# A hybrid attention block with a 2x2-block feed-forward: fewer block units, one adding transfer for each, and elementwise work moved from GpSimd to VectorE

## The chip, the core and the metric

The kernel runs on one core of a Trainium2 chip. It is one launch; its time is the device time of that core in microseconds (us). In the profile, PE is TensorE, DVE is VectorE, ACT is ScalarE, POOL is GpSimd and SP is the queue that issues most transfers. Each engine works through its own list of instructions; what stands behind a waiting one in that list is late with it.

## What is computed

One layer of a hybrid block on 512 tokens with 1024 channels, in fp32. Four mixers read the normed input, their outputs are gated and merged, and a gated feed-forward with 2816 hidden columns follows:

```
h = rms_norm(x, attn_norm);  proj = h @ w_in          # split into q, k, v, gates of four mixers
y_fox   = fox_attention(norm(fq), norm(fk), fv, ff)   # 4 heads, decayed causal softmax
y_conv  = cb * conv1d(cc * cu)                        # width 3, per channel
y_mlstm = sigmoid(mo) * norm(mlstm(mq, mk, mv, ...))  # 4 heads, chunks of 64
y_swa   = swa_attention(norm(sq), norm(sk), sv)       # 8 heads, window 128
merged  = sum over the four of sigmoid(gate_i) * (y_i @ w_i_out)
x = x + merged @ w_merge_out
h = rms_norm(x, ffn_norm)
x = x + (silu(h @ w_gate) * (h @ w_up)) @ w_down
```

## The kernel before

All tokens stand in the free dimension: a tile is 128 channels by 512 tokens. Every fp32 operand is split into a high part `hi` and a remainder `lo` (`split`: ACT copies `hi`, DVE subtracts for `lo`), and each product is made of three matmuls (`mm3`): hi by hi, hi by lo, lo by hi. A projection (`proj`) of 128 output columns is 8 such triples, 24 matmuls of 512 columns.

The weights are one stream `w_str` of tiles of 128 x 1024 fp32 in the order of use. SP loads them into six buffers `wraw`; `w_split` splits each into `whi`/`wlo` (four buffers each, so two or three tiles ahead of their use).

The order of the program is: token projections `psn` on the raw input with the sums of squares `ssq`; `fk`, `fq` of the fox mixer (on `xg`, the input times the norm's gain, without the norm's factor); the conv mixer's `pcu`, `pcc`, `pcb` (on `xn`, the normed input, made by `normed_input`); the eight gate and output pairs of conv (`gconv`, `oconv`) with the fox attention mixed in; `sk`, `sq` of the window mixer, each normed per head (`head_normed`); `gfox`/`ofox` with the window attention mixed in; `pmv`, `pmk`, `pmq`, `pmo`; `gswa`; `gmlstm`; the merge `mg`; and the feed-forward. Attention runs as a background generator: `tick`, called once for each triple, advances it every `pace["period"]` triples. Projections and outputs share four PSUM buffers (`ps_mm`), taken in turn: `gconv` of the first output block takes the buffer that `pcb` of p = 0 held, and so waits until that has been read.

The feed-forward has 22 units of 128 hidden columns. A direct unit (`plain_unit`, the first three) is two projections, 48 matmuls of 512 columns. A block unit (the other 19) sees K (two halves), tokens (two halves) and gate/up as a 2x2 block product and makes it with 7 half products instead of 8: 7 x 4 x 3 = 84 matmuls of 256 columns (`product`). Its four weight sums t1 to t4 come from transfers that add as they write: `ff_load` adds into `ta` (t1 and t3), `ff_t2` copies t1 on ACT and adds a third tile into the copy, `ff_t4` copies t2 on ACT and adds a fourth. These adding transfers are issued from POOL (`accum_op`). After units 0 to 7, 8 to 14 and 15 to 21 follows the down product of that part (`dn`): eight output blocks, each a sum over the part's units, times `r2`, added to `x2`. The tile scheduler places the instructions of each engine; its order is what the compiled program has.

The head of the kernel's tuning that the change touches, and the product of a block unit:

```
PLAIN = 3
...
PARTS = ((0, 8), (8, 7), (15, 7))
...
def product(ps, w, a, start, stop):
    for k in range(4):
        wb = slice(k * P, (k + 1) * P)
        (wh, wl), (ah, al) = w, left[a][k]
        nc.tensor.matmul(ps, wh[:, wb], ah, ...)
        nc.tensor.matmul(ps, wh[:, wb], al, ...)
        nc.tensor.matmul(ps, wl[:, wb], ah, ...)
```

## Time and profile before

| | us |
|---|---|
| median of 3 runs | 864.37 (861.04 to 865.3) |
| the profiled execution's own time | 867.11 |
| its span, first to last instruction | 865.4 |
| PE busy / DVE busy / ACT busy / POOL busy | 835.9 / 593.1 / 429.0 / 225.9 |

The span is 1.7 us shorter than the execution's own time; the profiled execution is 2.7 us above the median. PE's busy time is not a measure of its pace: matmuls overlap, so a stretch is PE at its pace only if the starts of its matmuls stand as close as they can. The mean granted clock of TensorE was 0.99 of full speed.

### The profile page before, as it was taken

What the parts mean: (1) busy time and instruction counts of PE and PEld (TensorE: products, weight loads), DVE (VectorE), ACT (ScalarE), POOL (GpSimd) and SP (SyncE); (2) the same over time, 40 slices, a digit from 0 to 9 for tenths busy, and PEclk for the clock granted to TensorE, in tenths of its full rate; (3) what the DMA queues carried; (4) which work ended last, traced back from release to release, by engine and by line L of the source; (5) the groups of instructions that cost most, each with busy time, mean ns of one, the idle gap of its engine ahead of it and who ended that gap; (6) DMA issues with size and microseconds to landing.
All of it is one profiled execution on the core that took longest, in us unless ns stands there. A gap on an engine that the chain in (4) does not pass through costs nothing.

```text
span 865.4 us, 12163 instructions
## 1 busy us (share of the span) xinstructions
PE 835.9 (97%) x4563; PEld 722.0 (83%) x4563; DVE 593.1 (69%) x933; ACT 429.0 (50%) x704; POOL 225.9 (26%) x220
## 2 busy tenths in 40 slices
...
GB/s 317 175 123 112 84 74 74 98 127 43 84 88 86 147 85 51 96 87 167 184 119 173 123 75 119 199 182 181 131 147 183 204 212 109 158 191 159 86 56 86
DMA packets 47215, 112.36 MB, mean 130 GB/s; under 512 B 4991, under 2 KB 8616, under 8 KB 47156
## 3 DMA queue, kind: packets, MB, share of 16 engines
...
q14 instruction: 23, 0.19, 0.1%
...
## 4 chain that ended last, share of the span: by engine, by line
PE 77%; DVE 8%; ACT 4%; DMA 4%; issue 3%; POOL 3%; SPq 0%; ACTq 0%; DVEq 0%; POOLq 0%
PE dn L136 5%; PE dn L134 5%; PE dn L135 5%; DMA fta<-in_w_str_dram 3%; PE fa L922 2%; DVE fl L140 2%; PE fc L921 2%; PE fc L920 2%; PE fc L922 2%; PE fa L920 2%; PE gswa L134 2%; PE fa L921 2%; PE gswa L135 2%; PE gswa L136 2%; PE gmlstm L134 2%
## 5 line engine op out<-in xcount | busy, mean ns | idle before, releaser
L140 DVE TENSOR_TENSOR wl<-wr,wh 128x1024 fp32r<-128x1024 f32 x79 | 106.9, 1353 | 40.2 <-ACT wh L139 37.5
L139 ACT CAST wh<-wr 128x1024 fp32r<-128x1024 f32 x79 | 82.7, 1047 | 60.3 <-PE gconv L135 8.6
L135 PE MATMUL dn<-al,dh 128*128 128x512 f32 x176 | 68.4, 389 | 0.0
L136 PE MATMUL dn<-ah,dl 128*128 128x512 f32 x176 | 68.0, 390 | 0.0
L134 PE MATMUL dn<-ah,dh 128*128 128x512 f32 x176 | 67.2, 389 | 0.0
L139 ACT CAST dh<-dr 128x896 fp32r<-128x896 f32 (+1 forms) x24 | 23.1, 977 | 55.9 <-DMA dr<-in_w_str_dram 18.8
L140 DVE TENSOR_TENSOR fl<-fr,fh 128x1024 fp32r<-128x1024 f32 x19 | 39.4, 2072 | 9.5 <-ACT fh L139 9.5
L922 PE MATMUL fc<-lh,fl 128*128 128x256 f32 x152 | 43.4, 285 | 2.1 <-DVE fl L140 2.1
L1005 POOL TENSOR_TENSOR ut<-ut,gt 128x512 f32<-128x512 f32 x19 | 30.2, 1591 | 54.5 <-DVE ut L1003 45.6
L140 DVE TENSOR_TENSOR dl<-dr,dh 128x896 fp32r<-128x896 f32 (+1 forms) x24 | 35.6, 1488 | 12.9 <-ACT dh L139 12.9
L920 PE MATMUL fc<-lh,fh 128*128 128x256 f32 x152 | 43.3, 285 | 0.6 <-ACT fh L139 0.6
L921 PE MATMUL fc<-ll,fh 128*128 128x256 f32 x152 | 43.3, 285 | 0.0
L920 PE MATMUL fb<-lh,fh 128*128 128x256 f32 x152 | 43.2, 285 | 0.0
L921 PE MATMUL fb<-ll,fh 128*128 128x256 f32 x152 | 43.1, 284 | 0.0
L922 PE MATMUL fb<-lh,fl 128*128 128x256 f32 x152 | 43.0, 284 | 0.0
L1049 DVE TENSOR_TENSOR o<-dn,r 128x512 f32<-128x512 f32 (+1 forms) x25 | 16.3, 666 | 35.1 <-PE dn L136 35.1
L136 PEld LDWEIGHTS dn<-ah,dl 128*128 128x128 f32 x176 | 33.0, 188 | 7.3 <-DVE dl L140 0.5
L135 PEld LDWEIGHTS dn<-al,dh 128*128 128x128 f32 x176 | 33.1, 188 | 6.7
L134 PEld LDWEIGHTS dn<-ah,dh 128*128 128x128 f32 x176 | 33.1, 188 | 6.6
L139 ACT CAST fh<-fr 128x1024 fp32r<-128x1024 f32 x19 | 19.9, 1047 | 27.5 <-PE fc L921 23.9
L1051 POOL TENSOR_TENSOR x<-x,o 128x512 f32<-128x512 f32 x16 | 27.6, 1734 | 22.4 <-DVE o L1049 22.4
L819 POOL DMA_DIRECT2D fta<-in_w_str_dram x19 | 17.4, 939 | 61.4 <-DMA fta<-in_w_str_dram 36.7
...
## 6 DMA issues: line engine op xcount, KB each, us to landing
...
fr<-in_w_str_dram SPq DMA_DIRECT2D x19, 256.0 KB, 3.2
fr<-in_w_str_dram POOLq DMA_DIRECT2D x19, 256.0 KB, 5.4
ftb<-in_w_str_dram POOLq DMA_DIRECT2D x19, 256.0 KB, 5.6
...
```

The lines of the kernel that those rows point to most:

```text
L134: nc.tensor.matmul(out, a[0], b[0], start=start, stop=False)
L135: nc.tensor.matmul(out, a[0], b[1], start=False, stop=False)
L136: nc.tensor.matmul(out, a[1], b[0], start=False, stop=stop)
L139: nc.scalar.copy(hi, src)
L140: nc.vector.tensor_tensor(lo, src, hi.bitcast(F32), op=ALU.subtract)
L819: nc.gpsimd.dma_start(ta, src[1].rearrange("p (i c) -> p i c", i=2), accum_op=ALU.add)
L920: nc.tensor.matmul(ps, wh[:, wb], ah, start=start and k == 0, stop=False, skip_group_check=True)
L921: nc.tensor.matmul(ps, wh[:, wb], al, start=False, stop=False, skip_group_check=True)
L922: nc.tensor.matmul(ps, wl[:, wb], ah, start=False, stop=stop and k == 3, skip_group_check=True)
L1005: nc.gpsimd.tensor_tensor(ut, ut, gt, op=ALU.mult)
L1049: nc.vector.tensor_tensor(o[:, c:c + n], ps[:, c:c + n], r2[:, c:c + n], op=ALU.mult)
L1051: nc.gpsimd.tensor_tensor(x2[d], x2[d], o, op=ALU.add)
```

## The change

- Of the 22 feed-forward units 13 are block units (W) and 9 direct (P), in four parts `PPPWWP`, `WWPWWP`, `WWPWW`, `PWWPW`; the down product follows each part, so there are 32 down blocks instead of 24, each over 6 or 5 units.
- A block unit has one adding transfer (into `ta`). t2 and t4 are sums on DVE (`src_t2`, `src_t4`); the two ACT copies and two adding transfers go.
- All weights, those of block units and of the down product too, go through one list of jobs, loaded up to six buffers ahead and split by `w_split`.
- Elementwise work of POOL goes to DVE: the sums of squares, the products by the norm, the gated sums `acc`, `ut * gt`, `x2 + o`, and half of the sums of the left blocks. The copies for the second half of a key stack go the other way, from DVE to a transfer issued by POOL (`k_stack`).
- The conv projections read `xg` (the norm's factor is applied later, `r_sq` and `rb_`), so the normed input is first needed by `gconv`, and its making is spread over more steps. The high part of a squared head comes from a second ACT square.
- The fox attention starts after the conv projections, and goes on through the projections of the window mixer.

The diff, cut to what is spoken of:

```diff
-PLAIN = 3
+PARTS = ("PPPWWP", "WWPWWP", "WWPWW", "PWWPW")
...
+    def load_b2(f):
+        def go(raw):
+            src = w_str[FF0 + 2 * f:FF0 + 2 * f + 2]
+            ta[f] = big.tile([P, 2, NT], F32, tag="ysw", name=f"fta{f}", bufs=4)
+            nc.sync.dma_start(ta[f], src[:, :, 0:NT].rearrange("i p c -> p i c"))
+            nc.sync.dma_start(raw.rearrange("p (i c) -> p i c", i=2), src[:, :, NT:].rearrange("i p c -> p i c"))
+            nc.gpsimd.dma_start(ta[f], src[1].rearrange("p (i c) -> p i c", i=2), accum_op=ALU.add)
+        return go
+    def src_t2(f, i):
+        def go():
+            raw = stream["raw"][i + 1]
+            nc.vector.tensor_tensor(raw[:, NT:], ta[f][:, 0], stream["raw"][i][:, NT:], op=ALU.add)
+            return raw
+        return go
+    def src_t4(f, i):
+        def go():
+            t = wk(f"ftb{f}")
+            nc.vector.tensor_tensor(t, stream["raw"][i + 1][:, NT:], stream["raw"][i][:, 0:NT], op=ALU.add)
+            return t
+        return go
...
+    f = 0
+    for part in PARTS:
+        f0 = f
+        for kind in part:
+            if kind == "P":
+                add_whole(FF0 + 2 * f)
+                add_whole(FF0 + 2 * f + 1)
+            else:
+                i = len(loads)
+                loads += [load_b2(f), load_b11(f)]
+                jobs += [(i, src_t2(f, i), 2), (i, lambda f=f: ta[f].rearrange("p i c -> p (i c)"), 2),
+                         (i, src_raw(i), 2), (i, src_t4(f, i), 1)]
+            f += 1
+        for d in range(KO):
+            jobs.append((len(loads), src_raw(len(loads), (f - f0) * P), 0))
+            loads.append(load_cols((d * FB + f0) * P, (f - f0) * P))
...
-            nc.gpsimd.tensor_tensor(ssq, ssq, sq, op=ALU.add)
+            nc.vector.tensor_tensor(ssq, ssq, sq, op=ALU.add)
...
-        nc.gpsimd.tensor_tensor(t, t, rb_, op=ALU.mult)
+        nc.vector.scalar_tensor_tensor(
+            t, t, col[:, C_AN + ko:C_AN + ko + 1], rb_, op0=ALU.mult, op1=ALU.mult)
         h, l = s_tile(f"xnh{ko}", F32R), s_tile(f"xnl{ko}", F32R)
-        scaled_split(h, l, t, col[:, C_AN + ko:C_AN + ko + 1])
+        split(h, l, t)
         xn.append((h, l))
...
-            nc.vector.tensor_copy(a[oth], a.bitcast(F32)[own])
+            nc.gpsimd.dma_start(a[oth], a[own])
             nc.vector.tensor_tensor(b[own], src[own], a.bitcast(F32)[own], op=ALU.subtract)
-            nc.vector.tensor_copy(b[oth], b.bitcast(F32)[own])
+            nc.gpsimd.dma_start(b[oth], b[own])
...
-        nc.vector.tensor_copy(h, sq)
-        nc.gpsimd.tensor_tensor(l, sq, h.bitcast(F32), op=ALU.subtract)
+        if src is None:
+            nc.vector.tensor_copy(h, sq)
+        else:
+            nc.scalar.activation(h, src, AF.Square)
+        nc.vector.tensor_tensor(l, sq, h.bitcast(F32), op=ALU.subtract)
...
-        nc.gpsimd.tensor_tensor(qg, qg, sq, op=ALU.mult)
+        nc.vector.tensor_tensor(qg, qg, sq, op=ALU.mult)
...
-        ps = proj(f"pcu{p}")
+        ps = proj(f"pcu{p}", xg)
         u = wk(f"cu{p}")
-        nc.scalar.copy(u, ps)
-        ps = proj(f"pcc{p}")
+        nc.vector.tensor_tensor(u, ps, r_sq, op=ALU.mult)
+        ps = proj(f"pcc{p}", xg)
         z = wk(f"cz{p}")
         nc.vector.tensor_tensor(z, ps, u, op=ALU.mult)
-        if p == 0:
-            pace["period"] = TUNE["fox_p"]
-            background.append(fox_attention())
         cw = [col[:, C_CW + 2 * k + p:C_CW + 2 * k + p + 1] for k in range(3)]
         nc.scalar.activation(u, z, AF.Copy, scale=cw[2])
         nc.vector.scalar_tensor_tensor(u[:, 1:], z[:, :-1], cw[1], u[:, 1:], op0=ALU.mult, op1=ALU.add)
         nc.vector.scalar_tensor_tensor(u[:, 2:], z[:, :-2], cw[0], u[:, 2:], op0=ALU.mult, op1=ALU.add)
-        ps = proj(f"pcb{p}")
+        nc.vector.tensor_tensor(u, u, rb_, op=ALU.mult)
+        ps = proj(f"pcb{p}", xg)
         nc.vector.tensor_tensor(u, ps, u, op=ALU.mult)
...
-                nc.gpsimd.tensor_tensor(acc[d], acc[d], t, op=ALU.add)
+                nc.vector.tensor_tensor(acc[d], acc[d], t, op=ALU.add)
...
+    flush()
+    pace["period"] = TUNE["fox_p"]
+    background.append(fox_attention())
     gated("conv", False)
-    flush()
+    pace["mixed"] = True
...
+    pace["mixed"] = False
+    while background:
+        bg()
...
-    def ff_load(f):
-        if not PLAIN <= f < FB:
-            return
-        r1 = big.tile([P, 2, NT], F32, tag="wraw", name=f"fr{f}", bufs=W_RAW)
-        rr = big.tile([P, 2, NT], F32, tag="wraw", name=f"fs{f}", bufs=W_RAW)
-        ta = big.tile([P, 2, NT], F32, tag="ysw", name=f"fta{f}", bufs=4)
-        src = w_str[FF0 + 2 * f:FF0 + 2 * f + 2]
-        nc.sync.dma_start(ta, src[:, :, 0:NT].rearrange("i p c -> p i c"))
-        nc.sync.dma_start(r1[:, 0], src[0, :, 0:NT])
-        nc.sync.dma_start(rr, src[:, :, NT:].rearrange("i p c -> p i c"))
-        nc.gpsimd.dma_start(ta, src[1].rearrange("p (i c) -> p i c", i=2), accum_op=ALU.add)
-        ff_raw[f] = [r1, ta, rr]
-    def ff_t2(f):
-        if not PLAIN <= f < FB:
-            return
-        r1, ta, _ = ff_raw[f]
-        nc.scalar.copy(r1[:, 1], ta[:, 0])
-        nc.gpsimd.dma_start(r1[:, 1], w_str[FF0 + 2 * f + 1, :, NT:], accum_op=ALU.add)
-    def ff_t4(f):
-        if not PLAIN <= f < FB:
-            return
-        t4 = wk(f"ftb{f}")
-        nc.scalar.copy(t4, ff_raw[f][0][:, 1])
-        nc.gpsimd.dma_start(t4, w_str[FF0 + 2 * f, :, NT:], accum_op=ALU.add)
-        ff_raw[f].append(t4.rearrange("p (i c) -> p i c", i=1))
...
+    def block_unit(f):
         bA, bB = ps_mm(f"fa{f}")[:, 0:HT], ps_at(f"fb{f}")[:, 0:HT]
         bC, bD = ps_mm(f"fc{f}")[:, 0:HT], ps_at(f"fd{f}")[:, 0:HT]
         gt, ut = wk(f"gt{f}"), wk(f"ut{f}")
         t1, t2 = slice(0, HT), slice(HT, NT)
+        product(bA, w_take(), "a11", True, True)
         nc.scalar.copy(gt[:, t2], bA)
+        product(bB, w_take(), "s2", True, True)
         nc.vector.tensor_tensor(ut[:, t1], gt[:, t2], bB, op=ALU.add)
+        product(bC, w_take(), "s1", True, True)
+        w_t3 = w_take()
+        product(bA, w_take(), "a12", False, True)
+        nc.vector.tensor_tensor(gt[:, t1], bA, r2[:, t1], op=ALU.mult)
+        product(bB, w_t3, "s3", False, True)
         nc.vector.tensor_tensor(ut[:, t2], gt[:, t2], bB, op=ALU.add)
+        w_22 = w_take()
+        product(bD, w_take(), "a22", True, True)
         nc.vector.tensor_tensor(gt[:, t2], ut[:, t2], bD, op=ALU.add)
         nc.vector.tensor_tensor(gt[:, t2], gt[:, t2], r2[:, t2], op=ALU.mult)
+        nc.scalar.activation(gt, gt, AF.Silu)
         nc.vector.tensor_tensor(ut[:, t2], bC, ut[:, t2], op=ALU.subtract)
+        product(bC, w_22, "s4", False, True)
         nc.vector.tensor_tensor(ut[:, t1], bC, ut[:, t1], op=ALU.subtract)
+        nc.vector.tensor_tensor(ut, ut, gt, op=ALU.mult)
+        return ut
...
-                    nc.gpsimd.tensor_tensor(x2[d], x2[d], o, op=ALU.add)
+                    nc.vector.tensor_tensor(x2[d], x2[d], o, op=ALU.add)
```

In the order of the compiled program the number of PE's rows goes from 4549 to 4333, six times the 36 matmuls by which a block unit has more than a direct one. Three places:

First, DVE before the first `gconv`. `cu<-pcb` is the read that frees its PSUM buffer; it is row 95 before and row 112 after, while `v_a`, the start of the norm's factor, is row 23 before and row 29 after. Before:

```order
L140 TENSOR_TENSOR wl_960<-wr_672,wh_959 128x1024
L475 SCALAR_TENSOR_TENSOR fq1v<-fq1m,epsv 128x512
L714 SCALAR_TENSOR_TENSOR cu_731<-cz_788,col,cu_731 128x510
L445 CAST fk1a_758<-fk1a_758 64x512
L446 TENSOR_TENSOR fk1b_759<-fk1g,fk1a_758 64x512
L445 CAST fk1a_764<-fk1a_764 64x512
L446 TENSOR_TENSOR fk1b_765<-fk1g,fk1a_764 64x512
L716 TENSOR_TENSOR cu_731<-pcb_793,cu_731 128x512
```

After (`xs`, `xnl` are the normed input, which now ends here):

```order
L142 TENSOR_TENSOR wl_955<-wr_692,wh_954 128x1024
L142 TENSOR_TENSOR xnl_758<-xs_754,xnh_757 128x512
L800 SCALAR_TENSOR_TENSOR cu_689<-cz_729,col,cu_689 128x510
L142 TENSOR_TENSOR xnl_788<-xs_784,xnh_787 128x512
L799 SCALAR_TENSOR_TENSOR cu_833<-cz_868,col,cu_833 128x511
L559 SCALAR_TENSOR_TENSOR fq1v<-fq1m,epsv 128x512
L153 SCALAR_TENSOR_TENSOR fk1s<-fk1s,fk1v 128x512
L801 TENSOR_TENSOR cu_689<-cu_689,r_b 128x512
L142 TENSOR_TENSOR wl_984<-wr_736,wh_983 128x1024
L800 SCALAR_TENSOR_TENSOR cu_833<-cz_868,col,cu_833 128x510
L154 SCALAR_TENSOR_TENSOR fk1s<-fk1s,fk1y 128x512
L803 TENSOR_TENSOR cu_689<-pcb_735,cu_689 128x512
```

Between `v_a` and that read DVE has 73 rows before and 84 after: three more weight splits of 1024, eighteen more operations of 512 columns with two tensors, ten casts of 512 fewer.

Second, POOL in the feed-forward. Before, about one unit:

```order
L834 DMA ftb_6100<-in_w_str_dram 128x512
L1005 TENSOR_TENSOR ut_5849<-ut_5849,gt_5848 128x512
L819 DMA fta_6248<-in_w_str_dram 128x1024
L834 DMA ftb_6232<-in_w_str_dram 128x512
L827 DMA fr_6114<-in_w_str_dram 128x512
```

After, the whole feed-forward is the thirteen `fta` rows, the first four of which stand right behind the last row of the mixers:

```order
L722 AFFINE_SELECT me_2_3658<-me_2_3658 128x128
L722 AFFINE_SELECT me_3_3687<-me_3_3687 128x128
L186 DMA fta_4569<-in_w_str_dram 128x1024
L186 DMA fta_4666<-in_w_str_dram 128x1024
L186 DMA fta_5232<-in_w_str_dram 128x1024
```

Third, DVE in a block unit. Before (`fl` are splits, the `ut` product is on POOL):

```order
L140 TENSOR_TENSOR fl_3_6361<-ftb_6232,fh_3_6360 128x512
L1000 TENSOR_TENSOR gt_6376<-fa_6372,r_4607 128x256
L1003 TENSOR_TENSOR ut_6245<-fc_6242,ut_6245 128x256
L140 TENSOR_TENSOR fl_0_6412<-fr_6114,fh_0_6411 128x1024
L993 TENSOR_TENSOR ut_6377<-gt_6376,fb_6373 128x256
L140 TENSOR_TENSOR fl_1_6456<-fta_6116,fh_1_6455 128x1024
L995 TENSOR_TENSOR gt_6376<-ut_6377,fd_6375 128x256
L140 TENSOR_TENSOR al_6369<-ut_6245,ah_6368 128x512
```

After (`ftb` is the new sum t4, and L1000 is the product that POOL made):

```order
L209 TENSOR_TENSOR ftb_5038<-wr_4720,wr_4665 128x512
L142 TENSOR_TENSOR wl_5037<-ftb_5038,wh_5036 128x512
L989 TENSOR_TENSOR gt_5004<-fa_5000,r_4612 128x256
L999 TENSOR_TENSOR ut_4877<-fc_4874,ut_4877 128x256
L1000 TENSOR_TENSOR ut_4877<-ut_4877,gt_4876 128x512
L142 TENSOR_TENSOR wl_5060<-wr_4753,wh_5059 128x1024
L991 TENSOR_TENSOR ut_5005<-gt_5004,fb_5001 128x256
```

A block unit has on DVE three splits of 1024 and one of 512, seven operations of 256, and the split of its result, as before, and now also two sums and one product of 512.

## Rows read from the trace of the kernel before

**Rows 1.** The page: busy time of each engine, share of the span, instructions.

```profile
PE 835.9 (97%) x4563; PEld 722.0 (83%) x4563; DVE 593.1 (69%) x933; ACT 429.0 (50%) x704; POOL 225.9 (26%) x220
```

**Rows 2.** What PE waited for: us in total, times, longest us.

```profile
PE fa L922 <- DVE fl L140: 5.3, 5, 1.2
PE fa L920 <- ACT gt L987: 3.1, 1, 3.1
```

**Rows 3.** Timeline of PE in the feed-forward: start us, us, instruction.

```profile
501.20 0.39 PE L134 MATMUL fg<-x2h,wh 128*128 128x512 f32 x1
...
518.01 0.39 PE L134 MATMUL fu<-x2h,wh 128*128 128x512 f32 x1
...
523.45 0.39 PE L134 MATMUL fg<-x2h,wh 128*128 128x512 f32 x1
...
584.15 0.28 PE L920 MATMUL fc<-lh,fh 128*128 128x256 f32 x1
...
587.03 0.28 PE L920 MATMUL fa<-x2h,fh 128*128 128x256 f32 x1
...
860.77 0.39 PE L136 MATMUL dn<-ah,dl 128*128 128x512 f32 x1
```

**Rows 4.** Stretches: us; busy PE, PEld, DVE, ACT, POOL; clock; DMA share; GB/s.

```profile
34.50:95.60 61.10, 56.15 (x242) 43.80 (x241) 55.52 (x74) 37.77 (x61) 24.76 (x17) 0.97 0.39 131
...
207.00:234.00 27.00, 23.18 (x103) 18.52 (x102) 19.10 (x35) 17.57 (x31) 9.21 (x7) 0.94 0.19 59
234.00:501.00 267.00, 267.00 (x1292) 224.54 (x1291) 184.38 (x349) 137.68 (x259) 54.81 (x58) 1.00 0.37 115
```

**Rows 5.** DVE by form, 533 to 866 us: busy us, mean ns; idle before, releaser.

```profile
L140 DVE TENSOR_TENSOR fl<-fr,fh 128x1024 fp32r<-128x1024 f32 x18 | 38.1, 2119 | 9.5 <-ACT fh L139 9.5
...
L140 DVE TENSOR_TENSOR fl<-fs,fh 128x1024 fp32r<-128x1024 f32 x19 | 23.1, 1214 | 4.0 <-ACT fh L139 4.0
...
L1049 DVE TENSOR_TENSOR o<-dn,r 128x512 f32<-128x512 f32 x23 | 15.6, 688 | 31.8 <-PE dn L136 31.8
...
L1003 DVE TENSOR_TENSOR ut<-fc,ut 128x256 f32<-128x256 f32 x19 | 8.1, 424 | 28.5 <-PE fc L922 28.5
```

**Rows 6.** DVE by form, 28 to 98 us.

```profile
L140 DVE TENSOR_TENSOR wl<-wr,wh 128x1024 fp32r<-128x1024 f32 x10 | 13.1, 1313 | 5.8 <-ACT wh L139 5.7
L144 DVE SCALAR_TENSOR_TENSOR xnl<-xs,col,xnh 128x512 fp32r<-128x512 f32 x8 | 9.4, 1195 | 0.5 <-ACT xnh L143 0.4
...
L350 DVE TENSOR_TENSOR g_u<-g_c,g_m 4x512 f32<-4x512 f32 x1 | 1.8, 1802 | 0.0
L713 DVE SCALAR_TENSOR_TENSOR cu<-cz,col,cu 128x511 f32<-128x511 f32 x1 | 1.7, 1677 | 0.0
L152 DVE SCALAR_TENSOR_TENSOR fq0s<-fq0s,fq0y 128x512 f32<-128x512 f32 x1 | 1.7, 1674 | 0.0
...
L460 DVE CAST fk0u<-fk0s 128x512 fp32r<-128x512 f32 x1 | 0.4, 417 | 0.0
```

**Rows 7.** POOL by form, the whole span.

```profile
L1005 POOL TENSOR_TENSOR ut<-ut,gt 128x512 f32<-128x512 f32 x19 | 30.2, 1591 | 54.5 <-DVE ut L1003 45.6 <-issue 8.9
...
L827 POOL DMA_DIRECT2D fr<-in_w_str_dram x19 | 19.9, 1045 | 43.3 <-ACT fr L826 38.4 <-ACT gt L987 2.7 <-DMA dr<-in_w_str_dram 2.0
...
L256 POOL TENSOR_TENSOR ssq<-ssq,xsq 128x512 f32<-128x512 f32 x7 | 12.0, 1709 | 7.0 <-ACT xsq L255 6.6
```

**Rows 8.** Timeline of DVE, 221 to 228.5 us.

```profile
221.99 2.20 DVE L140 TENSOR_TENSOR wl<-wr,wh 128x1024 fp32r<-128x1024 f32 x1 [0.25 <-ACT wh L139]
```

**Rows 9.** Timeline of POOL in the same stretch.

```profile
221.82 1.29 POOL L744 TENSOR_TENSOR acc<-acc,tfox 128x512 f32<-128x512 f32 x1 [3.26 <-DVE tfox L743]
```

**Rows 10.** Timeline of ACT at the start of gfox.

```profile
216.67 1.28 ACT L148 ACT_TABLE_LOAD   x1 [2.98 <-DVE sq3v L473]
```

**Rows 11.** ACT by form, 533 to 866 us.

```profile
L826 ACT COPY fr<-fta 128x512 f32<-128x512 f32 x15 | 9.3, 619 | 18.9 <-DMA fta<-in_w_str_dram 11.2 <-DVE fl L140 5.2 <-DVE dl L140 2.4
```

**Rows 12.** DMA issues: KB each, median us to landing.

```profile
fr<-in_w_str_dram POOLq DMA_DIRECT2D x19, 256.0 KB, 5.4
```

More of the change, by code (lines that the diff above doesn't have):

```diff
@@ L167, in w_split, with load_whole, load_cols, go @@
-    def w_split():
-        i = stream["split"]
-        if i >= n_w:
-            return
-        stream["split"] = i + 1
-        while stream["raw"] <= min(i + W_RAW - 1, n_w - 1):
-            w_load()
+    loads, jobs = [], []
+    stream = {"load": 0, "job": 0, "raw": {}, "ready": []}
+    sums, ta = {}, {}
+    def load_whole(t):
+        def go(raw):
+            nc.sync.dma_start(raw, w_str[t])
+        return go
+    def load_cols(at, n):
+        def go(raw):
+            done = 0
+            while done < n:
+                t, o = divmod(at + done, 2 * NT)
+                m = min(n - done, 2 * NT - o)
+                nc.sync.dma_start(raw[:, done:done + m], w_str[DN0 + t, :, o:o + m])
+                done += m
+        return go
@@ L174, in w_split @@
+    def w_split():
+        i = stream["job"]
+        stream["job"] = i + 1
+        first, src, halves = jobs[i]
+        while stream["load"] < min(first + W_RAW, len(loads)):
+            n = stream["load"]
+            stream["load"] = n + 1
+            stream["raw"][n] = big.tile([P, 2 * NT], F32, tag="wraw", name=f"wr{n}", bufs=W_RAW)
+            loads[n](stream["raw"][n])
         hi = big.tile([P, 2 * NT], F32R, tag="whi", name=f"wh{i}", bufs=W_BUF)
         lo = big.tile([P, 2 * NT], F32R, tag="wlo", name=f"wl{i}", bufs=W_BUF)
-        split(hi, lo, stream["raws"][i])
@@ L190 @@
     background, deferred = [], []
-    pace = {"period": 4, "count": 0}
+    pace = {"period": 4, "count": 0, "mixed": False}
     def later(steps, fn):
@@ L211, in tick @@
         pace["count"] += 1
-        if pace["count"] >= pace["period"] and not deferred:
+        if pace["count"] >= pace["period"] and (pace["mixed"] or not deferred):
             pace["count"] = 0
@@ L688 @@
     gr, bl = gate_rows(), swa_bias_line()
-    for n in (6, 14, 22, 30, 38):
+    for n in (8, 18, 28, 40, 50):
         later(n, lambda: next(gr, None))
-    later(40, lambda: next(bl, None))
+    later(56, lambda: next(bl, None))
+    for hh in range(FOX_H):
+        later(60 + 2 * hh, lambda hh=hh: negc.append(bcast_row(f"negc{hh}", hh)))
     for ko in range(KO):
```

212 lines of the change are left out of this document (67 added, 145 removed).

## The prediction

> **What bounds the kernel now.** The page comes first: PE is busy 97% of the span, DVE 69% [rows 1]. Busy PE is not PE at its pace, so the second view is PE's timeline. 24 direct matmuls of 512 columns start within 523.45 - 518.01 = 5.44 us, 0.2267 each; 24 block matmuls of 256 columns within 587.03 - 584.15 = 2.88 us, 0.120 each [rows 3]. From the first `fg` to the last `dn` are 860.77 - 501.20 = 359.6 us. At those paces the work is 144 direct matmuls of units 0 to 2, 528 of the down product and 2 of the norm, 674 x 0.2267 = 152.8 us, and 19 units x 84 x 0.120 = 191.5 us: 344.3. So PE loses about 15.3 us in the feed-forward and is its bound for the rest. What it waits for is the third view: in sum 5.3 us a split by DVE, 3.1 us an ACT copy [rows 2]; a restart at a lower clock and smaller gaps are the rest. Both engines are late for one reason each. DVE takes 2.12 us for the split of `fr` and 1.21 for that of `fs`, of the same size [rows 5]; a split of 2.20 us stands beside an operation of POOL with two tensors that starts 0.17 us earlier and lasts 1.29 [rows 8, 9]. ACT's copies wait 11.2 us for adding transfers [rows 11], with PE's copies behind them.
>
> Two more places are left by the view of stretches. From 34.5 to 95.6 us, where the conv projections are, PE is idle 61.1 - 56.2 = 4.9 us and its clock is 0.97 of full speed, worth 0.03 x 61.1 = 1.8 us; DVE is busy 55.5 of the 61.1. From 207 to 234 us, at the start of `gfox`, PE is idle 3.8 us at a clock of 0.94 (1.6 us): 5.4 us lost. From 234 to 501 us PE is busy without a gap [rows 4].
>
> **The change, part by part.** *Fewer block units.* Six units go from 84 x 0.120 = 10.08 us to 48 x 0.2267 = 10.88 [rows 3]: +0.8 each, **+4.8 us**. This is certain, and the only part that adds PE work. (The Trainium skill, TensorE: Matmul & The Clock Gate, Back-to-back issue gap, gives columns over 2.4 GHz plus 2.5 ns, 216 and 109 ns; by it the six would cost 7.3 us and the forecast be 853.5. The trace is slower at both widths, 227 and 120, and decides.)
>
> *What DVE has in a unit.* A block unit has three splits of 1024 (1.21), one split, two new sums, the new product and the split of its result at 0.69, and seven operations of 0.42 [rows 5]: 3.6 + 3.5 + 2.9 = 10.0 us, beside 10.08 of PE. A direct unit has two splits and three operations of 512, 4.5 us beside 10.9. Two to one makes 24.5 of 31.0 us: a pair of block units is level with PE, a direct unit or the down product pays back. In a down block of six units DVE has a shorter split (between 0.69 and 1.21) and two operations of 0.69, at most 2.6 us beside 18 x 0.2267 = 4.1; that hides the eight more down blocks of the fourth part, whose matmuls stay 528. POOL's product of 1.59 us [rows 7] becomes 0.69, and what it added to the splits, 0.9 us on `fr` alone, goes.
>
> *The adding transfers.* 38 of 57 go, and all 38 ACT copies. The first four of the thirteen left stand in POOL's order right behind the mixers, some 100 us before their use; each later one can start when `ta` of the unit four before is split, over 20 us ahead. ACT so waits for none. What can be late next is t2 on DVE, which waits for `ta` with all of DVE's order behind it.
>
> So of the 15.3 us lost in the feed-forward I leave 3 us, about 0.5 for each of the six adjacent pairs: bounds 0 (all hidden) and 8 (a level DVE loses half of what was lost). Feed-forward: 4.8 - 15.3 + 3 = **-7.5 us**, from -10.5 to -2.5.
>
> *Before the gates.* The conv projections no longer wait for the normed input, but the first `gconv` waits for the read of the first `pcb`, and DVE reaches it after 84 rows instead of 73. The load: three more splits (3.6), eighteen more operations at 0.69 (12.4), ten casts fewer (4.2 at 0.42) is +11.8 us; what POOL added goes: 8 x 0.51 on `xnl`, 10 x 0.10 on the splits, and 1.1, 1.0, 1.0 on three single rows, 8.2 us [rows 5, 6]. DVE is then busy 55.5 + 11.8 - 8.2 = 59.1 us. It starts some 1.5 us earlier, since the seven sums of squares take 0.69 on DVE and not 1.71 on POOL [rows 7], 7.1 us in all, of which DVE's own order gives back most (bounds 0 and 3). With idle time between none and the 5.6 us of before, the read is done at 33.0 + 59.1 + 0 to 5.6 = 92 to 98 us, instead of 95.6. PE alone would be there some 10 us earlier, so it waits for DVE. I take the middle of the idle time, 95: **-1 us** (-5 to +3).
>
> *Start of gfox.* `tfox` on ACT stands behind the norm of the last `sq`, for which ACT waited 2.98 us on DVE [rows 10]; DVE stood beside POOL's products there. The table loads, 1.28 us each, stay. I take **-4** of the 5.4 us (0 to -5.4).
>
> *At nothing.* The gated sums and the rest of the moved work between 234 and 501 us lie beside PE: DVE is busy 184 of 267 us there, and 24 sums at 0.69 add 17. The longer fox attention takes the same matmuls. The ACT squares are nine at about 0.62, ACT being busy 50%. The key copies on POOL's queue (issue 1.05 us, landing 5.4 us for the nearest kind [rows 7, 12]) are some 10 us a stack against 1.7 before: cover is the 16 matmuls of `psq` and the `gfox` block behind the sum, over 10 us; without it each stack is some 8 us of wait.
>
> Sum: -7.5 - 1 - 4 = -12.5, with -1 for the short delays that POOL's work leaves elsewhere: -13.5. The profiled execution of 867.1 would be 853.6; the median of 864.4, which is 2.7 lower, **851**.
>
> **Rivals.** (a) *Nothing new waits*: -10.5 - 5 - 5.4 = -21, **843**. For it: every wait in rows 2 has its cause removed. Against: DVE is level in pairs of block units.
>
> (b) *The two places ahead gain nothing*, DVE being as late as before at `gconv` and `gfox`: only -7.5, **857**. For it: DVE's 59 us in a stretch where it was busy 55.5.
>
> (c) *DVE is the bound in block units*, slower than before: t2, t4 and the product make 2.1 us more in each than before, in DVE's one order, where t2 may wait for its transfer. If each of 13 units loses 2 us, 26, the sum is 4.8 - 15.3 + 26 - 5 = +10.5, **875**. It decides against the change from (15.3 + 5 - 4.8) / 13 = 1.2 us per unit. For it: 10.0 beside 10.08. Against: before, with POOL's delays, DVE's load was no smaller and PE lost 15.3 / 19 = 0.8 per unit, with no direct units between.
>
> (d) *The key copies come late*, because POOL can't issue while DVE runs: the stack of `sk` would miss its 10 us of cover by some 8, and the time be **859**. Rows show an issue of 1.05 us beside a busy DVE, which speaks against it, but none for a copy within SBUF. (The Trainium skill, SBUF — State Buffer, SBUF: two separate sides, says that a transfer issued by GpSimd can starve while VectorE holds the port that both share. No row here shows it.)
>
> **How the numbers follow.** My forecast has 0.57, own range 845 to 857; (a) 0.14, (b) 0.14, (c) 0.10, (d) 0.05. A measurement here can tell about 0.5%, 4.3 us: faster is below 860.1, slower above 868.7. Faster: 0.55 of the forecast, all of (a), 0.10 of (b), 0.03 of (d), less a little for what I have not seen, 0.79. Slower: 0.09, nearly all of (c). Same: 0.12. Leaving out the lower third of (a), (c) and the edge of (d) gives 841 to 862.
>
> **What the profile would show.** The splits `wl` at 1.21 us in the feed-forward, no PE wait above 1 us there, and first `fg` to last `dn` 352 us. The first `gconv` between 92 and 98 us, waiting for DVE. PE's idle time at `gfox` under 2 us. Wrong would be: gaps of PE at every pair of block units with DVE without a pause (c), DVE waiting for `fta`, or `gconv` beyond 100 us.

## The result and the profile after

The changed kernel takes **840.92 us** (median of 4 runs, 840.54 to 841.49), the kernel before 864.84 beside it: a ratio of 0.972 (0.967 to 0.977). The forecast was 851 with a range of 841 to 862; the time lies 0.1 us below the range, at rival (a), and the gain of 24 us is almost twice the 13.5 forecast.

The page of the changed kernel, busy time of each engine; it answers to [rows 1]. POOL has lost nearly all its work, DVE is no busier than before:

```profile
PE 831.2 (99%) x4347; PEld 712.2 (85%) x4347; DVE 582.4 (69%) x1019; ACT 402.6 (48%) x664; POOL 36.5 (4%) x79
```

What PE waited for in the changed kernel, whole list (us in total, times, longest), against [rows 2]. No split of a block unit and no ACT copy is left in it:

```profile
PE warm_ps L304 <- DVE warm L301: 1.3, 1, 1.3
PE psn L136 <- ACT wnh L141: 1.2, 1, 1.2
PE fo L617 <- DVE fx_0l L142: 0.7, 1, 0.7
PE dn L136 <- ACT ah L141: 0.5, 1, 0.5
PE fg L138 <- DVE wl L142: 0.4, 1, 0.4
PE oconv L136 <- ACT ych L141: 0.2, 1, 0.2
```

The time is best followed by the stretches between the first starts of some matmuls in PE's timeline (the column feed-forward ends at the start of the last `dn`). All runs of this study stand here, from their profiled executions; the experiments below read it.

| us | start to pcu | pcu to gconv | gconv to gfox | gfox to pmv | pmv to fg | feed-forward | span |
|---|---|---|---|---|---|---|---|
| before | 52.4 | 45.0 | 99.0 | 71.5 | 233.3 | 359.6 | 865.4 |
| after | 48.9 | 35.4 | 101.1 | 65.6 | 232.8 | 351.4 | 839.7 |
| change | -3.5 | -9.6 | +2.1 | -5.9 | -0.5 | -8.2 | -25.7 |
| conv_xn | 47.8 | 35.7 | 99.7 | 65.2 | 232.8 | 350.7 | 836.6 |
| pool_head | 52.3 | 41.0 | 100.7 | 67.1 | 232.9 | 350.9 | 850.1 |
| fox_early | 48.5 | 35.4 | 100.1 | 70.8 | 232.9 | 350.8 | 843.1 |
| late_read | 48.9 | 35.4 | 113.1 | 65.2 | 232.8 | 351.3 | 851.4 |
| pool_ffn | 48.7 | 35.4 | 101.1 | 65.5 | 232.8 | 353.2 | 841.7 |
| add_dma | 48.3 | 35.4 | 101.1 | 65.5 | 232.8 | 398.8 | 886.5 |
| w19 | 48.4 | 35.4 | 101.1 | 65.5 | 232.8 | 350.5 | 838.5 |
| b_no_pool | 48.6 | 42.5 | 103.7 | 65.2 | 233.2 | 357.4 | 855.3 |
| b_sums | 50.9 | 44.7 | 99.0 | 71.5 | 233.3 | 349.1 | 853.1 |
| b_np_sums | 48.2 | 41.4 | 106.0 | 65.2 | 233.3 | 350.2 | 850.1 |
| spread_back | 48.8 | 38.7 | 105.6 | 65.2 | 232.9 | 351.0 | 846.8 |
| k_dve | 49.2 | 35.4 | 103.9 | 67.3 | 232.9 | 351.1 | 844.4 |
| f_front | 48.2 | 37.0 | 99.5 | 65.2 | 233.2 | 349.7 | 837.5 |
| f_front_sq | 48.3 | 35.7 | 99.5 | 65.2 | 233.2 | 350.1 | 836.6 |
| f_late_t2 | 48.8 | 35.7 | 99.5 | 65.2 | 233.2 | 350.7 | 837.7 |
| conv_w16 | 47.4 | 35.7 | 99.7 | 65.2 | 232.8 | 352.0 | 837.7 |
| after_again | 48.0 | 35.4 | 101.1 | 65.5 | 232.8 | 351.4 | 838.8 |

Some fox attention moved from the second column into the third, so the two belong together: -7.5 us, and with the first column -11.0 up to `gfox`. There the forecast had -1. after_again is the changed kernel once more: against the row after, its first column differs by 0.9 us and the others by 0.1 at most, which is how far such columns can be trusted.

The stretches in columns 2, 4 and 6 (the last taken to the end of its final matmuls), of the kernel before (us; busy PE, PEld, DVE, ACT, POOL with counts; granted clock; DMA share; GB/s):

```profile
52.40:97.40 45.00, 40.05 (x169) 30.69 (x168) 42.21 (x52) 26.55 (x41) 16.38 (x11) 0.96 0.33 106
...
196.40:267.90 71.50, 67.68 (x323) 55.97 (x322) 57.56 (x141) 45.42 (x103) 21.00 (x15) 0.98 0.21 67
...
501.20:862.00 360.80, 348.85 (x2271) 319.71 (x2269) 239.76 (x309) 158.57 (x218) 108.45 (x105) 1.00 0.60 148
```

and of the changed kernel:

```profile
48.80:84.30 35.50, 35.50 (x159) 28.55 (x158) 34.86 (x50) 24.39 (x38) 2.83 (x5) 1.00 0.46 140
...
185.40:251.00 65.60, 65.55 (x324) 55.05 (x323) 56.98 (x148) 46.64 (x105) 3.03 (x8) 1.00 0.26 81
...
483.80:837.00 353.20, 350.84 (x2055) 311.06 (x2053) 233.63 (x356) 128.91 (x171) 7.83 (x9) 1.00 0.38 109
```

In the first pair DVE makes 52 operations in 42.2 us of 45.0, and then 50 in 34.9 of 35.5: it is full in both, but each operation is shorter, and PE has no gap left. In the second pair PE's 3.8 us of idle time are gone, and its clock is at its upper level throughout.

The step that failed shows in two places of the trace. PE's timeline of the changed kernel (start us, us):

```profile
84.06 0.39 PE L138 MATMUL pcb<-xh,wl 128*128 128x512 f32 x1
84.28 0.39 PE L136 MATMUL gconv<-xnh,wh 128*128 128x512 f32 x1
...
91.83 0.50 PE L136 MATMUL oconv<-ych,wh 128*128 128x512 f32 x1 [0.22 <-ACT ych L141]
```

and DVE's:

```profile
90.44 0.68 DVE L803 TENSOR_TENSOR cu<-pcb,cu 128x512 f32<-128x512 f32 x1
```

The first `gconv` starts 0.22 us behind the last `pcb`, at pace, and 6.2 us ahead of the read for which it was said to wait. It stood so in the kernel before too, PE's timeline:

```profile
97.20 0.39 PE L136 MATMUL pcb<-xnh,wl 128*128 128x512 f32 x1
97.42 0.39 PE L134 MATMUL gconv<-xnh,wh 128*128 128x512 f32 x1
```

No wait of `gconv` stands in what PE waited for, before or after. What the words ahead of the prediction say of the buffer of `pcb` p = 0 and the first `gconv` is wrong. What PE did wait for there, 0.5 us, is `ych` at the first `oconv`; in the kernel before ACT made it at 102.82 us, 7.2 us behind the end of that read, since two pieces of the split of `fq1q` stood ahead of it and ACT had waited 2.40 us for the product `fq1g` on POOL.

### The profile page after: what moved, and what is told of

Read it like the earlier page. It is cut to its first block, busy times and chain, and to the rows that moved or that the text cites. A ratio compares the mean times of both kernels' runs of the same rounds, so it can differ in the third digit from the quotient of the medians.

```text
span 839.7 us, 11529 instructions
## 1 busy us (share of the span) xinstructions
PE 831.2 (99%) x4347; PEld 712.2 (85%) x4347; DVE 582.4 (69%) x1019; ACT 402.6 (48%) x664; POOL 36.5 (4%) x79
## 4 chain that ended last, share of the span: by engine, by line
PE 95%; DVE 1%; DMA 1%; ACT 1%; issue 0%; SPq 0%; DVEq 0%
PE dn L138 5%; PE dn L136 5%; PE dn L137 5%; PE fg L138 2%; PE fu L138 2%; PE fg L136 2%; PE fu L137 2%; PE fu L136 2%; PE fg L137 2%; PE gconv L136 2%; PE gswa L136 2%; PE gmlstm L136 2%; PE gconv L137 2%; PE gswa L138 2%; PE gswa L137 2%; PE mg L136 2%
## 5 line engine op out<-in xcount | busy, mean ns | idle before, releaser
L141 ACT CAST wh<-wr 128x1024 fp32r<-128x1024 f32 (+2 forms) x149 | 147.0, 992 | 184.5 <-PE dn L137 41.1
L142 DVE TENSOR_TENSOR wl<-wr,wh 128x1024 fp32r<-128x1024 f32 (+2 forms) x149 | 170.7, 1148 | 38.7 <-ACT wh L141 38.3
L136 PE MATMUL dn<-ah,wh 128*128 128x512 f32 x176 | 67.6, 391 | 0.5 <-ACT ah L141 0.5
L137 PE MATMUL dn<-al,wh 128*128 128x512 f32 x176 | 68.0, 389 | 0.0
L138 PE MATMUL dn<-ah,wl 128*128 128x512 f32 x176 | 68.0, 391 | 0.0
L136 PEld LDWEIGHTS dn<-ah,wh 128*128 128x128 f32 x176 | 33.0, 188 | 7.7 <-ACT ah L141 1.0
L138 PEld LDWEIGHTS dn<-ah,wl 128*128 128x128 f32 x176 | 33.0, 188 | 7.2 <-DVE wl L142 0.5
L137 PEld LDWEIGHTS dn<-al,wh 128*128 128x128 f32 x176 | 33.1, 188 | 6.8
L962 PE MATMUL fb<-lh,wl 128*128 128x256 f32 x104 | 29.6, 284 | 0.0
L961 PE MATMUL fb<-ll,wh 128*128 128x256 f32 x104 | 29.5, 283 | 0.0
```

The costliest lines, as they stand in the source:

```text
L136: nc.tensor.matmul(out, a[0], b[0], start=start, stop=False)
L137: nc.tensor.matmul(out, a[0], b[1], start=False, stop=False)
L138: nc.tensor.matmul(out, a[1], b[0], start=False, stop=stop)
L141: nc.scalar.copy(hi, src)
L142: nc.vector.tensor_tensor(lo, src, hi.bitcast(F32), op=ALU.subtract)
L961: nc.tensor.matmul(ps, wh[:, wb], al, start=False, stop=False, skip_group_check=True)
```

## The experiments

Each edit is against the changed kernel, or, in the labels that begin with b_ and f_, against the kernel before. Times are medians of 4 runs unless said; the kernel before took 863 to 865 beside them.

**late_read.** The failed step, tested by itself.

```diff
         nc.vector.tensor_tensor(u, u, rb_, op=ALU.mult)
+        if p == 0:
+            for _ in range(10):
+                nc.vector.tensor_tensor(u, u, u, op=ALU.max)
```

> The changed kernel with ten idle operations of 512 columns (the maximum of a tile with itself) on DVE ahead of the read of the first pcb, which by DVE's order comes some 9 to 10 us later, near 100 us. The step of the prediction (the first gconv waits for this read): first gconv from 84.3 to about 101, the time 856 to 858. Theory A (the second gconv and the first oconv wait for it, the first gconv doesn't): first gconv stays at 84.3, the second goes from 92.2 to about 101, the time 847 to 850.

852.24. PE's timeline:

```profile
84.30 0.39 PE L136 MATMUL gconv<-xnh,wh 128*128 128x512 f32 x1
...
102.35 0.80 PE L136 MATMUL oconv<-ych,wh 128*128 128x512 f32 x1 [10.73 <-ACT ych L141]
```

and DVE's:

```profile
95.88 5.04 DVE L804 TENSOR_TENSOR cu<-cu 128x512 f32<-128x512 f32 x7
100.95 0.69 DVE L806 TENSOR_TENSOR cu<-pcb,cu 128x512 f32<-128x512 f32 x1
```

The read came 10.5 us later, the first `gconv` as before, and PE lost 10.7 us at the first `oconv`, whose input `ych` is made from that read. So the read is on the path (in the changed kernel PE waits 0.22 us behind it), but one block of `gconv` later than the prediction had it: theory A, with a price above its upper bound of 850.

**conv_xn.** The conv projections read the normed input again.

```diff
-        ps = proj(f"pcu{p}", xg)
+        ps = proj(f"pcu{p}")
         u = wk(f"cu{p}")
-        nc.vector.tensor_tensor(u, ps, r_sq, op=ALU.mult)
+        nc.scalar.copy(u, ps)
...
-        nc.vector.tensor_tensor(u, u, rb_, op=ALU.mult)
...
-    "ml_p": 4, "ml_v": 3, "ml_n": 8, "warm": 7, "xn_0": 14, "xn_p": 6,
+    "ml_p": 4, "ml_v": 3, "ml_n": 8, "warm": 7, "xn_0": 3, "xn_p": 3,
```

> The changed kernel, with its conv projections on the normed input again, made as early as before; the rest stays. Theory A, PE's loss ahead of the first gconv was its wait for the normed input itself, whatever makes it: before, 6.8 us between 52 and 72 us. Then 4 to 7 us come back: 845 to 848. Rival B, the normed input was late only because POOL multiplied it and slowed the splits: with all of it on DVE it is in time, under 1.5 us: 841 to 842.5. The step of the prediction (first gconv waits for the read of the first pcb, DVE's load decides) would give less DVE work here (two products of 512 fewer, 1.4 us) and a time no later than 841.

838.51 (837.94 to 839.25): 2.4 us faster than the changed kernel, below theories A and B; the third line, less work on DVE, gave no time later than 841 and holds, though its wait of `gconv` doesn't. PE doesn't wait for a piece of the normed input here, so the rewrite saves no wait and costs DVE four products. In the kernel before PE did wait for such pieces. POOL's multiplying is not the whole of that: with POOL's work moved and nothing reordered (b_np_sums) PE still waits 2.2 us for one at `pcu`, and with the order changed too (f_front) 0.6.

**pool_head.** The head's elementwise work on POOL again (four operations, this is one, and the split that goes with one of them; the projections stay on the raw input).

```diff
-            nc.vector.tensor_tensor(ssq, ssq, sq, op=ALU.add)
+            nc.gpsimd.tensor_tensor(ssq, ssq, sq, op=ALU.add)
```

> The changed kernel with the elementwise work of the head on POOL again: the sums of squares, the products of the normed input, the low part of a squared head, and its product by the norm; the conv projections still read the raw input. Theory A: 1 to 3 us, by the token projections and gfox, and the first gconv not over 2 us later: 842 to 844. Rival B: POOL's work is the cause, and 6 to 9 us come back: 847 to 850.

851.56, 10.6 us slower, beyond rival B; 8.7 us of it up to `gfox`, 1.5 in the stretch behind. DVE by form, 28 to 98 us, in this run (busy us, mean ns):

```profile
L142 DVE TENSOR_TENSOR wl<-wr,wh 128x1024 fp32r<-128x1024 f32 x10 | 14.6, 1458 | 10.5 <-ACT wh L141 10.4
L146 DVE SCALAR_TENSOR_TENSOR xnl<-xs,col,xnh 128x512 fp32r<-128x512 f32 x8 | 7.7, 968 | 0.2 <-ACT xnh L145 0.2
```

and in the changed kernel:

```profile
L142 DVE TENSOR_TENSOR wl<-wr,wh 128x1024 fp32r<-128x1024 f32 x12 | 14.6, 1218 | 2.1 <-ACT wh L141 2.0
...
L142 DVE TENSOR_TENSOR xnl<-xs,xnh 128x512 fp32r<-128x512 f32 x8 | 5.5, 682 | 0.0
```

**spread_back.** The head's deferred steps as in the kernel before.

```diff
-    for n in (8, 18, 28, 40, 50):
+    for n in (6, 14, 22, 30, 38):
...
-                    lag=(18, 56)[p])
+                    lag=18)
```

> The changed kernel with the steps at which the head's deferred work is called as before: both pairs of fk and fq 18 steps after their projection instead of 18 and 56, the gate rows at 6 to 38 and the broadcast rows with them; the fox attention still starts behind the conv projections. Theory A, moving POOL's work alone left 6.1 us lost by the conv projections and 9.4 by gconv, and this spreading took most of them: +5 to +10, 846 to 851. Rival: the later start of the fox attention or the single adding of parts did it, 0 to 2: 841 to 843.

848.77, 7.9 us slower, theory A. PE's timeline shows what DVE and ACT come late with, the normed input, for which DVE now has less room:

```profile
92.70 0.50 PE L137 MATMUL gconv<-xnl,wh 128*128 128x512 f32 x1 [1.31 <-DVE xnl L142]
...
98.35 0.79 PE L136 MATMUL gconv<-xnh,wh 128*128 128x512 f32 x1 [3.72 <-ACT xnh L141]
```

**k_dve.** The copies of the key stacks on DVE.

```diff
-            nc.gpsimd.dma_start(a[oth], a[own])
+            nc.vector.tensor_copy(a[oth], a.bitcast(F32)[own])
```

> The changed kernel with the copies of the key stacks on DVE again, 12 operations of 0.42 us, in the place of transfers that POOL issues. If the transfers came late (rival d of the prediction): -8 to -2, 833 to 839. If they are hidden: 0 to +1, 841 to 842.

846.54: 5.6 us slower, where at most 1 was expected. The edit puts 20 copies back, 12 of them, 5.0 us at 0.42, for the stacks needed up to `gfox`; 3.2 us are lost up to the first `gfox` and 1.7 in the stretch behind it. PE's timeline, at the same `oconv` as above:

```profile
94.50 0.50 PE L136 MATMUL oconv<-ych,wh 128*128 128x512 f32 x1 [2.60 <-ACT ych L141]
```

**fox_early.** The fox attention behind the first `pcc`, as before.

```diff
         nc.vector.tensor_tensor(z, ps, u, op=ALU.mult)
+        if p == 0:
+            pace["period"] = TUNE["fox_p"]
+            background.append(fox_attention())
...
-    flush()
-    pace["period"] = TUNE["fox_p"]
-    background.append(fox_attention())
     gated("conv", False)
```

> The changed kernel with the fox attention begun behind the first pcc, as before. Before, PE lost 2.9 us at the first score matmuls (84 to 92 us). Theory A, that loss belongs to the early start: +2 to +3, 843 to 844. Rival: the stacks are ready earlier now, 0 to 1: 841 to 842.

844.74, 3.8 us slower, the size of theory A in another place: up to `gfox` the run is 1.4 us shorter (0.9 of it is within the scatter of the first column), and the loss is in the stretch behind it (70.8 against 65.6), where PE waits 2.8 us for the second square of `sq2` on ACT. Why the order of ACT there comes out otherwise was not followed up.

**pool_ffn.** The unit's product and the sum into `x2` on POOL.

```diff
-        nc.vector.tensor_tensor(ut, ut, gt, op=ALU.mult)
-        return ut
+        nc.gpsimd.tensor_tensor(ut, ut, gt, op=ALU.mult)
+        return ut
```

> The changed kernel with two operations of the feed-forward on POOL again: the product of each unit's result and the sum into x2. Theory A, POOL's two-tensor operations slow DVE's splits by about 1 us each and PE waits for them: 13 block units, 2 to 6 us: 843 to 847, with splits of 1024 above 1.6 us beside POOL. Rival: direct units and down blocks between give DVE enough room, 0 to 1: 841 to 842.

843.41, the lower end of theory A. DVE by form from 500 us: the splits are slowed to 1.47 us on the mean of all, and PE's feed-forward is only 1.8 us longer.

```profile
L142 DVE TENSOR_TENSOR wl<-wr,wh 128x1024 fp32r<-128x1024 f32 x38 | 55.7, 1465 | 4.0 <-ACT wh L141 4.0
```

**add_dma.** t2 and t4 by an ACT copy and an adding transfer, within the one stream of jobs.

```diff
-            nc.vector.tensor_tensor(raw[:, NT:], ta[f][:, 0], stream["raw"][i][:, NT:], op=ALU.add)
+            nc.scalar.copy(raw[:, NT:], ta[f][:, 0])
+            nc.gpsimd.dma_start(raw[:, NT:], w_str[FF0 + 2 * f + 1, :, NT:], accum_op=ALU.add)
```

> The changed kernel with t2 and t4 made by an ACT copy and an adding transfer again, within the new stream of jobs. Theory A, these transfers are late and ACT and PE stand behind them: 4 to 9 us: 845 to 850. Rival: the new stream asks for them early enough, and DVE has two operations of 0.69 us fewer in each block unit: -1 to +1, 840 to 842.

881.87 (877.25 to 888.32), 41 us slower than the changed kernel and 2% slower than before. What ACT waited for:

```profile
ACT wh L141 <- DMA ftb<-in_w_str_dram: 67.1, 13, 7.1
```

Every one of the 13 units waits for the transfer of t4, since the stream asks for a sum only when its split is next. The kernel before asked one unit ahead and hid most of them. The single stream and the sums on DVE belong together.

**w19.** Nineteen block units again.

```diff
-PARTS = ("PPPWWP", "WWPWWP", "WWPWW", "PWWPW")
+PARTS = ("PPPWWW", "WWWWWW", "WWWWW", "WWWWW")
```

> The changed kernel with 19 block units behind three direct ones, in four parts (PPPWWW, WWWWWW, WWWWW, WWWWW); all else as changed. Six units go from 10.88 to 10.08 us of PE: -4.8. Theory A, DVE is level with PE in a run of block units (10.0 beside 10.08 us) and PE loses at most 3: 836 to 840. Rival, DVE is the bound in a run: every unit loses over 0.8 us and the time is 842 to 852.

840.51 (838.78 to 842.41): no difference, between the two theories. PE's own work falls to 344.3 us, its stretch to 350.5: it loses 6.2 us and not 2.3, so six more block units cost 0.65 each in waits, where they save 0.80. Of the 6.2, PE's waits by name are 2.5 us for splits on DVE and 1.1 for ACT's `ah`. That fits DVE being level with PE in a run of block units, as worked out; the rest has no name in the view. The mix buys next to nothing.

**b_no_pool.** In the kernel before, all two-tensor operations of POOL to DVE (nine lines), nothing else.

```diff
-                nc.gpsimd.tensor_tensor(acc[d], acc[d], t, op=ALU.add)
+                nc.vector.tensor_tensor(acc[d], acc[d], t, op=ALU.add)
```

> The kernel before, with nothing changed but that its two-tensor operations on POOL (sums of squares, norm products, gated sums, half of the left sums, unit products, sums into x2) are on DVE. Theory A, POOL's slowing of DVE carries about half of the loss: 5 to 7 us in the feed-forward, 4 to 6 at gfox, 2 to 4 ahead of gconv: 849 to 854. Rival: DVE, with 19 block units in runs and more work, is late itself: 860 to 868.

856.28, between theory A and its rival. `gfox` gives back 6.3 us, more than in the changed kernel: POOL was all of it. Up to `gfox` it is 196.4 to 194.8. The feed-forward gives 2.2 only: PE's waits for splits fall from 7.4 to 0.6 us, but one of ACT's copies waits 6.9 us for the adding transfer into `ta`, and PE behind it:

```profile
565.17 0.58 PE L920 MATMUL fc<-lh,fh 128*128 128x256 f32 x1 [4.94 <-ACT fh L139]
```

**b_sums.** In the kernel before, t2 and t4 on DVE in the place of copies and transfers, POOL's work kept.

```diff
-        nc.scalar.copy(r1[:, 1], ta[:, 0])
-        nc.gpsimd.dma_start(r1[:, 1], w_str[FF0 + 2 * f + 1, :, NT:], accum_op=ALU.add)
+        nc.vector.tensor_tensor(r1[:, 1], ta[:, 0], rr[:, 1], op=ALU.add)
```

> The kernel before with t2 and t4 as sums on DVE in the place of ACT's copies and the adding transfers; its work on POOL and its nineteen block units stay. Theory A, two separate causes in the feed-forward: the 8.1 us that PE loses between 540 and 580 us go, the 7.0 us between 660 and 800 us (splits beside POOL) stay: 855 to 859. Rival: DVE, with two operations more in every unit beside POOL's, gets later than the transfers were: 862 to 872.

855.23. The feed-forward takes 349.1 us, the shortest of all runs, with 19 block units and with POOL beside DVE. Theory A had the 7.0 us at the splits stay; they went too. The splits are still slow, DVE by form from 533 us:

```profile
L140 DVE TENSOR_TENSOR fl<-fr,fh 128x1024 fp32r<-128x1024 f32 x18 | 31.0, 1723 | 5.4 <-ACT fh L139 5.4
```

against 2.12 us in [rows 5]. The timelines show what differs. In the kernel before, one such split on DVE, POOL beside it, and PE's wait:

```profile
663.67 3.28 DVE L140 TENSOR_TENSOR fl<-fr,fh 128x1024 fp32r<-128x1024 f32 x1 [0.53 <-ACT fh L139]
...
663.00 1.54 POOL L827 DMA_DIRECT2D fr<-in_w_str_dram  x1
663.56 2.30 POOL L1005 TENSOR_TENSOR ut<-ut,gt 128x512 f32<-128x512 f32 x1
...
667.01 0.39 PE L922 MATMUL fa<-a11h,fl 128*128 128x256 f32 x1 [1.22 <-DVE fl L140]
```

and in this run:

```profile
656.61 2.02 DVE L140 TENSOR_TENSOR fl<-fr,fh 128x1024 fp32r<-128x1024 f32 x1 [0.54 <-ACT fh L139]
...
656.26 1.29 POOL L1003 TENSOR_TENSOR ut<-ut,gt 128x512 f32<-128x512 f32 x1 [1.10 <-DVE ut L1001]
```

The split ends 1.1 us behind the end of POOL's product in both. In the kernel before that product takes 1.3 us where POOL has paused ahead of it, and up to 2.31 where it follows POOL's issue of an adding transfer without a pause. PE's five waits at `fa` for a split, 5.3 us, are at splits of 2.67 to 3.28 us, each beside a product of the second kind (1.96 to 2.31 us). Each split less the wait behind it is 2.06 to 2.07 us: an estimate of what PE covers, by which a split of 2.0 costs nothing. So these five waits came with both, the product and the adding transfers on POOL, and they are gone under either edit. PE's long waits behind ACT's copies are gone only with the sums; one wait of 2.1 us for another split is left.

**b_np_sums.** The edits of the last two together.

> Both at once in the kernel before: no two-tensor operation on POOL, and t2 and t4 as sums on DVE; order, units and conv as before. Theory A, the two add: PE loses at most 4 us in the feed-forward, 846 to 850, and what is left to the changed kernel is the order of the work ahead of gfox. Rival, DVE is then the bound in runs of block units: over 0.8 us per unit, 856 or more.

849.16, in the range of theory A. The same row:

```profile
L140 DVE TENSOR_TENSOR fl<-fr,fh 128x1024 fp32r<-128x1024 f32 x18 | 21.9, 1219 | 2.9 <-ACT fh L139 2.9
```

The split is back at 1.22 us, and the feed-forward no shorter (350.2, a loss of 5.9 and not the 4 expected). The rest of the gain isn't here: up to `gfox` 195.6 us, against 185.4.

**f_front.** To that, the order: key copies by transfers, deferred steps spread, fox attention behind the conv projections and at the changed kernel's pace. The second square on ACT isn't in it. Conv on the normed input, 19 block units, three parts and two lists of weights stay as before.

```diff
+    flush()
+    pace["period"] = TUNE["fox_p"]
+    background.append(fox_attention())
     gated("conv", False)
-    flush()
+    pace["mixed"] = True
```

> The kernel before with: no two-tensor operation on POOL, t2 and t4 as sums on DVE, the key stacks' copies by transfers that POOL issues, the deferred steps spread as in the changed kernel, and the fox attention behind the conv projections. Nineteen block units, two lists of weights, conv on the normed input and three parts stay. Theory A, DVE's load and order are all of it: PE loses at most 6 us from pcu to gfox (16.8 with POOL's move and the sums alone), 837 to 841. Rival, the conv rewrite or the single stream is needed: 845 to 850.

839.21 (838.78 to 840.19), theory A: the whole gain of the change without its conv rewrite, its mix of units, its fourth part and its stream.

**f_front_sq.** With the second square on ACT.

```diff
-        nc.vector.tensor_copy(h, sq)
+        nc.scalar.activation(h, src, AF.Square)
```

> The same with the high part of a squared head from a second square on ACT, which takes nine casts of 0.42 us from DVE. Theory A, DVE sets the pace there: 0 to 4 us less than the run above. Rival, ACT stands on the path at gfox: 0 to 2 more.

838.69 (837.97 to 840.02): 0.5 us, within the spread of the runs; up to `gfox` it is 1.1 us for 3.8 us of casts taken off DVE. One wait is left in its feed-forward, 3.4 us of PE behind a split; DVE stands in t2 of a later unit ahead of it, timeline:

```profile
520.39 0.69 DVE L832 TENSOR_TENSOR fr<-fta,fs 128x512 f32<-128x512 f32 x1 [3.85 <-DMA fs<-in_w_str_dram]
```

**conv_w16, after_again.** conv_w16 is conv_xn with this:

```diff
-PARTS = ("PPPWWP", "WWPWWP", "WWPWW", "PWWPW")
+PARTS = ("PPPWWW", "WWPWWW", "WWPWW", "WWPWW")
```

> The changed kernel without its conv rewrite (which made the run of that edit 2.4 us faster than the changed kernel), and with 16 block units (PPPWWW, WWPWWW, WWPWW, WWPWW). Three units fewer on the direct way are -2.4 us of PE's pace; runs of three block units lose perhaps half of it, as 19 block units lost 3.9 of 4.8: 837 to 838.5. If runs of three already make DVE the bound: 839 to 841.

> The changed kernel as it is, on this chip, to compare the three others with: 840 to 842.

839.82 and 840.75. With runs of three block units PE loses 5.3 us of the feed-forward (352.0 less 346.7), near the 6.2 of w19, and the time is 1.3 us above that of conv_xn. By name 1.5 us of PE's waits there are for splits; that three in a row bring DVE level fits this, but isn't shown.

**f_late_t2.** f_front_sq with t2 called a step later; 5 runs.

```diff
-        ... (lambda: (ff_split(f, 1), ff_t2(f + 1))), last
+        ... (lambda: ff_split(f, 1)), last
...
             ff_split(f, 3)
+            ff_t2(f + 1)
             ff_t4(f + 1)
```

> The forward version with the second square (838.7), with the sum t2 of the next block unit called one step later, behind the last split of the unit. Theory A, DVE's 3.85 us in the sum ahead of its weights is the whole of the 3.4 us wait of PE and of the 1.3 us of slower matmuls behind it: 833.5 to 835.5. Rival, the weights come too late anyway and the wait moves to the sum's new place: 838 to 840.

838.29. The scheduler left the sum in its place in DVE's order, and it waits there as before (3.56 us), so the run tells nothing on the theory; whether that wait can be had is open.

## Why the prediction failed, step by step

**The step that failed is the sum "Before the gates", -1 us where -11.0 up to `gfox` was measured.** It rests on "the first `gconv` waits for the read of the first `pcb`" and on "PE alone would be there some 10 us earlier, so it waits for DVE". The estimate of DVE was near in its sum, not in its terms: its read of `pcb` ends at 91.1 us, forecast 92 to 98. DVE makes `v_a` at 29.7 us and not 34.6, so the earlier start is 4.8 us, where 1.5 was taken (0 to 3); it is then busy 55.2 us instead of the 59.1 worked out, and idle 6.2. The main error came behind that: the work that needs it is the first `oconv`, one block of `gconv` (7.6 us) behind, so PE took its 10 us. The wait was read from the code's buffers; the view of PE's waits [rows 2] had no such row, and PE's timeline of before had `gconv` behind `pcb` without a gap. A wait that no view shows should have had a chance, not the sum.

What gave the 11 us: DVE, busy 94 and 98% there, sets the pace with ACT behind it, and what loads it, slows it or orders it badly costs PE time. Undone singly, POOL's work costs 8.7 us up to `gfox` (10.6 in all), the spread of deferred steps 7.7 (7.9), the key copies 3.2 (5.6). These add to more than the gain, and so are no shares of it. It doesn't hold the other way: nine casts fewer, 3.8 us, gave 1.1 (f_front_sq). The three with the sums and the later fox attention are enough (f_front).

**Feed-forward: -8.2, forecast -7.5.** The size was right, the causes half right. "Both engines are late for one reason each" falls: the sums on DVE alone bring -10.5, POOL's move alone -2.2, both -9.4. The row of 2.12 us was true, but a split slowed by POOL's product alone, 2.0 us, is hidden; PE's waits at `fa`, 5.3 us, came at splits of 2.67 us and more, where POOL had issued an adding transfer just ahead of the product (b_sums). So the adding transfers stood behind both kinds of wait, at DVE's splits and at ACT's copies, and POOL's product behind the first only.

**Fewer block units: +4.8 of PE work, as forecast** (349.1 us of work, by the working of the prediction with 9 direct units; 351.4 less that is the 2.3 lost, forecast 3). They give 3.9 back in waits, so the mix is worth nothing. Rival (c) priced a block unit at 2 us, its point of decision at 1.2; each of the six more in w19 loses 0.65. Of the 57 adding transfers 44 go, not 38, as 13 are left; the sum doesn't use that count. The gap of 216 and 109 ns that the prediction takes from the Trainium skill (TensorE: Matmul & The Clock Gate, Back-to-back issue gap) is there that of a matmul by itself and not of a stream; the stream in [rows 3] has 227 and 120 ns, and no term rests on the page's.

**Start of gfox: -5.9, forecast -4 with a bound of -5.4.** The cause was right, POOL beside the norm chain (b_no_pool alone gives -6.3); the table loads stay and are hidden.

**At nothing: the key copies are hidden, but were worth 5.6 us.** Rival (d) feared them late. POOL issued each in 0.5 us and they landed in 2.2 to 4.1, as in the issues of the changed kernel (KB each, median us to landing):

```profile
fk0a<-fk0a POOLq DMA_DIRECT2D x2, 128.0 KB, 2.5
...
fk1a<-fk1a POOLq DMA_DIRECT2D x2, 128.0 KB, 4.1
...
ska<-ska POOLq DMA_DIRECT2D x2, 128.0 KB, 2.8
```

What DVE is spared was counted, but in the sum that failed: ten casts, 4.2 us, set off there against DVE's new work.

**What the profile was to show.** Right: splits in the feed-forward at 1.22 us, no wait of PE above 0.5 us there, 351.4 us for the 352 given, and 0.05 us of PE's idle time at `gfox`. Wrong: the first `gconv`, at 84.3 us and waiting for nothing.

**The chances.** (a), nothing new waits, gave 843 and had 0.14; its -5 came from the sum that failed and was too small by 6 us; its -5.4 at `gfox` was near the -5.9 measured.
